# A two-layer hybrid encoder trunk: the output projection's second weight sum moved to VectorE, two stored gates fetched earlier, and three attention steps moved

## The chip, the cores and the metric

The kernel runs on one core of one Trainium2 chip. The metric is the device time of one launch in microseconds: the median of three runs. Beside it stands one execution under the hardware profiler, from which all rows of the profile come. A core has five engines, each of which works through its own list of instructions in order: TensorE (PE, with its weight loads as PEld), VectorE (DVE), ScalarE (ACT), GpSimd (POOL) and SyncE (SP), which here only issues DMAs. The engines wait for one another through semaphores. The lists are made ahead of time by a scheduler, from the order in which the code names the operations.

## The reference

The input is x with 512 rows of 1024 numbers. Two layers are applied. Each has a mixer with three branches and one output projection, and then a gated feed-forward block. Cut to what matters here:

```python
h = x @ w_in[l]                                  # 1024 -> all q, k, v and gates
o_a = retention(...)                             # branch 0: chunkwise retention
o_b = chunk_attention(...)                       # branch 1: softmax over a band of chunks, 8 heads of 64
o_c = diff_attention(...)                        # branch 2: softmax 1 - lam * softmax 2, 4 heads
g = sigmoid(gates + b_merge[l])                  # 3 x 1024 gates for each row
merged = g[0] * (o_a @ w_branch_a[l]) + g[1] * (o_b @ w_branch_b[l]) + g[2] * (o_c @ w_branch_c[l])
mix = merged @ w_out[l]
x = layer_norm(alpha * x + mix)
u_gate, u_up = split(x @ w_ffn_in[l])
x = layer_norm(alpha * x + (silu(u_gate) * u_up) @ w_ffn_out[l])
```

All of it is float32.

## The kernel before

**Products.** Each float32 operand is a pair hi and lo of the type float32r, and a product is three matmuls (`mm3`, L122 to L124: hi by hi, lo by hi, hi by lo). Making the pair is work for two engines: ScalarE casts the high half, VectorE subtracts it from the source for the low half (activations: L106/L108 and L112/L114; weights: L154/L155 and L271/L272). A block of weights passes through a staging tile `st` (four buffers) into `wh` and `wl` (three buffers each): blocks are fetched three ahead of use (`AHEAD`), and a block's cast can begin when the block three before it has been used up. A block is 24 matmuls of 512 columns for a unit of the output projection, and 24 or 48 for the others.

**Units.** The mixer is a list of units, `(u_gate(1, 0), [...], [...])` and so on. A unit loads one block of weights, computes two tiles, and calls `between()` after each; each call runs the next group of steps in the unit's lists. Steps named s_ are the small work of the branches. `u_dqk(h)` projects the queries and keys of one head pair of the differential branch, q first, then one group, then k, then the rest of the groups. `u_gate(br, i)` and `u_branch(br, i)` compute two tiles each of gates and branch outputs.

**The branches' steps.** `s_c1(h)` makes the scores of head h of the chunked attention in four PSUM banks (psc, L422/L423), adds a bias table and takes the maximum on VectorE (L437), exponentiates on ScalarE (L439), and normalises on VectorE (L910, L914). `s_c2(h)` transposes the result on TensorE (ptr, L452, ten transposes) and splits it into a pair (cP). `s_c3(h)` multiplies by v (pco, L939), and ScalarE and VectorE read the bank (cos L941, cot L942). `s_d0` to `s_d4` do the same for the differential branch: `s_d0(h, 1)` ends with the difference of the two softmaxes (L979 to L985, dE), `s_d2(h)` transposes dE, `s_d3(h)` multiplies by v, `s_d4(h)` turns the result. The eight PSUM banks rotate: a new tile waits until the tile that held its bank has been read.

**The gates.** A gate tile is th. Those of branch 0 and the pair (2, 0) are computed long before use (`EARLY`), stored to DRAM, and fetched again. In `u_branch` each tile's fetch (L1081) is issued by SP in the unit that uses it, and VectorE then computes (th + 1) * pt (L1083) and adds it to the branch sum (L1087). Sums of four tiles and quarter sums of them (s12, s43, m1, m2: `s_mleft` L294/L295, `s_mright` L304/L305) become the pairs for the output projection.

**The output projection** is done with seven products of quarter matrices instead of eight, called m1, m2, y, v, x, g, h in the order of use. Their weights are sums of quarters of w_out, each quarter 1 MB. Class `Chain` makes the sums along one staging tile `a`: m1 takes the first quarter, and then an accumulate DMA, issued by POOL (`more`, L178), adds the second quarter in place; y takes that sum, a second accumulate adds the fourth quarter; x takes it, a third accumulate adds the third quarter; h takes that. v and m2 load the fourth and third quarters as they are, and g's sum is made apart (`ahead_c`). The accumulate can start only when both ScalarE and VectorE have read `a` for the block before. The residual rows z (8 loads from x, L459) are updated from each product (L1141, L1143); the statistics for the norm follow (L478, L495, L497).

**SP's queue** takes the loads in the order in which the units are written, with weight loads three blocks ahead of use. A load whose staging buffer is not yet free holds up all that is queued behind it.

Of the kernel before, what the change touches and what calls it, by code (L numbers as in the profile page):

```python
# [56 lines left out]
def trunk(ctx, tc, x_in, xT_in, w_in, ret_norm_g, da_norm_g, lq1, lk1, lq2, lk2, w_a, w_b, w_c, b_merge, w_out,  # L57
# [133 lines left out]
    class Chain(Halves):  # L191
# [21 lines left out]
        def v(self):  # L213
            return self.block(self.load(1, 1))

        def h(self):
            return self.block(self.__dict__.pop("a"))

    class Close(Halves):

# [395 lines left out]
    def layer(l):  # L616
# [282 lines left out]
        def s_c1(h):  # L899
            def fn():  # L900
                if h == 0:
                    bias_table(0)
                if h + 1 < CA_HEADS:
                    bias_table(h + 1)
                tb = ctb.pop(h)
                nc.vector.memset(tb[0:64, 0:64], -NEG)
                E = [g(name="cE") for _ in range(3)]
                sums = softmax_num(cqk[h // 2], h % 2, tb, E)
                r = small.tile([P, NT], F32, tag="rec", name="rec")
                nc.vector.reciprocal(r, sums)  # L910
                for nt in range(NT):
                    pk, c = PACK[NT - 1 - nt]
                    e = E[pk][:, c:c + P * (nt + 1)]
                    nc.vector.tensor_scalar_mul(e, e, r[:, nt:nt + 1])  # L914
                cE[h] = E
            return fn

        def s_c2(h):
            def fn():
                cP[h] = triangle("cP")  # L920
                transpose_triangle(cE.pop(h), cP[h])
            return fn

        def s_c3(h):
            def fn():
                p, j = divmod(h, 2)
                if j == 0:
                    ob[p] = g(name="cot")
                o_ = ob[p]
                pT = cP.pop(h)  # L930
                ps = bank("pco")
                for mt in range(NT):
                    b, o = PACK[mt]
                    w = S - P * mt
                    vt, c = v_of(cv, mt, h, 64)
                    hi = (ps[:, P * mt:], vt[:, c:c + P], pT[b].hi[:, o:o + w])
                    lo = (ps[:64, P * mt:], vt[:, c:c + 64], pT[b].lo[:, o:o + w])
                    for x in ((hi, lo) if mt == 0 else (lo, hi)):
                        nc.tensor.matmul(*x, start=mt == 0 and x is hi, stop=mt == NT - 1 and x is hi)  # L939
                t = g(name="cos")  # L940
                nc.scalar.copy(t[:64], ps[64:128])  # L941
                nc.vector.tensor_add(o_[64 * j:64 * j + 64], ps[:64], t[:64])  # L942
                if j:
                    ob[p] = Pair("ob")
                    split(ob[p], o_)
            return fn
# [5 lines left out]
        def u_dqk(h):  # L952
            def fn(wt):
                if "cd" not in tabs:
                    tabs["cd"], tabs["sd"], tabs["mask"] = g(name="cosd"), g(name="sind"), g(name="mask")
                    nc.sync.dma_start(tabs["cd"], rope_da[0])
                    nc.sync.dma_start(tabs["sd"], rope_da[1])
                    nc.vector.memset(tabs["mask"], 0.0)
                    nc.vector.memset(tabs["mask"][0:64, 0:64], -NEG)
                dqk[h] = QK()  # L960
                dqk[h].set_q(rotary(proj_T(xT, wt, 0), tabs["cd"], tabs["sd"], 32), -DA_DH ** -0.5)
                between()
                dqk[h].set_k(rotary(proj_T(xT, wt, P), tabs["cd"], tabs["sd"], 32))
            return [([wcols(DQ + P * h, P), wcols(DK + P * h, P)], KT)], fn
# [99 lines left out]
        def u_gate(br, i):  # L1064
# [3 lines left out]
                    between()  # L1068
            return [(cols_of(W, GATE + D * br, br, i), KT)], fn

        def u_branch(br, i):
            w = (w_a, w_b, w_c)[br][l]
            nk = w.shape[0] // P

            def fn(wt):
                act = (oa, ob, oc)[br]
                for j, d in enumerate(tiles(br, i)):
                    t = th.pop((br, d))
                    if (br, i) in EARLY:
                        away, t = t, g(name="th")  # L1080
                        nc.sync.dma_start(t, away)  # L1081
                    ps = proj_T(act, wt, P * j, nk=nk)
                    nc.vector.scalar_tensor_tensor(t, t, 1.0, ps, op0=ALU.add, op1=ALU.mult)  # L1083
                    if br == 0:
                        acc[d] = t
                    else:
                        nc.vector.tensor_add(acc[d], acc[d], t)  # L1087
                    if br == 2 and j == 0:
                        q = mq[d] = Quarters()
                        pr = HalfPair("m1")  # L1090
                        split(pr, acc[d][:, q.A], scale=0.5)
                        q.put("m1", pr, q.A)
                    elif br == 2:
                        pr = Pair("m2")
                        split(pr, acc[d], scale=0.5)
                        mq[d - 4].put("m2", pr, q.A)
                        mq[d - 4].put("h", pr, q.B)
                    between()
            return [(cols_of(w, 0, br, i), nk)], fn
# [53 lines left out]

        def out_items():

            hv = Chain(w_out[l], 0, 4)
            w = {}

            def it(name, i, hf, op, last=False, whole=False):
                def fn(wt):  # L1160
                    on = {"x": "m1", "g": "m1", "h": "m1", "v": "y"}.get(name, name)
                    for j in range(2):
                        t = 2 * i + j
                        w[on, j] = product(mq, name, j, wt, w.pop((on, j), None))
                        plus(x1, t, hf, w[on, j], op, last)
                        if name in ("m2", "v", "h"):
                            w.pop((on, j))
                        if whole:
                            x1["n"].normalise(t)
                        between()  # L1170
                return [getattr(hv, name)], fn

            add, sub = ALU.add, ALU.subtract
            return {"c": hv.ahead_c, "m1": it("m1", 0, 0, add), "m2": it("m2", 0, 0, add, True), "y": it("y", 1, 1, add),
                    "x": it("x", 0, 1, sub, True, True), "v": it("v", 0, 1, add), "g": it("g", 1, 1, sub, True),
                    "h": it("h", 1, 0, add, True, True)}
# [25 lines left out]
        for (specs, fn), *groups in start + [  # L1202
            (w["x"], [p["a"]]), (u_gate(0, 3),), (w["g"],), (w["h"], [p["c"]]),
            (p["m1"], [s_dh(0)]), (p["y"], [], [s_r1(0)]), (p["v"], [s_dh(1)]), (p["m2"], [], [s_r1(1)]),
            (p["x"], [q["a"]]), (u_rqk(rq, RQ, 1),), (p["g"], [q["c"]]), (p["h"],),
            (q["m1"], [], [s_r2(0)]), (q["y"], [s_r2(1)]), (u_rqk(rk, RK, 1), [], [s_r3(0)]),
            (q["v"], [s_dh(2)], [s_r3(1)]), (q["m2"], [], [s_r1(2)]), (q["x"], [s_dh(3)]), (u_cqk(0), [], [s_r1(3)]), (q["g"],), (q["h"],),
            (u_gate(2, 0), [s_r2(2)], [s_r2(3), s_r3(2)]), (u_cqk(1), [s_r3(3)] + c(0)[0], c(0)[1]),
            (u_branch(0, 0), c(1)[0] + [v_back(cv)], c(1)[1]), (u_branch(0, 1), *c(2)), (u_cqk(2), *c(3)),
            (u_branch(0, 2), *c(4)), (u_cqk(3), *c(5)), (u_branch(0, 3), *c(6)),   # L1210
            (u_dqk(0), [s_c3(5), s_c2(6), s_c1(7)]), (u_gate(1, 0), [s_c3(6)], [s_c2(7)]),
            (u_dqk(1), [v_back(dv), s_c3(7)] + d(0)[1]), (u_branch(1, 0), *d(1)),
            (u_gate(1, 1), [], d(2)[0] + d(2)[1]), (u_branch(1, 1), *d(3)), (u_dqk(2),),
            (u_gate(1, 2), *d(4)), (u_branch(1, 2), *d(5)), (u_dqk(3),),
            (u_gate(1, 3), *d(6)), (u_branch(1, 3), *d(7)), (u_gate(2, 1), [s_d4(2)], [s_d2(3)]),
            (u_gate(2, 2), [s_d3(3)], [rows_in, s_d4(3)]),
            (u_branch(2, 0), [], [s_mleft(0)]), (u_branch(2, 1), [], [s_mleft(1)]), (u_gate(2, 3), [s_mright(0)], [s_mright(1)]),
            (u_branch(2, 2), [o["c"]]), (u_branch(2, 3), [], [s_mleft(2), s_mleft(3)]),
            (o["m1"], [s_mright(2)]), (o["m2"], [s_mright(3)]), (o["y"],), (o["v"],), (o["x"], [norm_rows]),
            (o["g"], [], [s_turned(0)]), (o["h"],),  # L1220
        ]:
            item(specs, fn, *groups)
# [237 lines left out]
```

## Time and profile before

| | |
|---|---|
| median of 3 runs | 1918.4 us (1915.35 to 1918.87) |
| the profiled execution, its own time | 1918.99 us |
| its span, first to last instruction | 1917.2 us |
| mean granted TensorE clock | 0.990 |
| DVE busy | 1390.2 us, 73% |
| mean weight cast (L271) and low half (L272) of a 1 MB block | 1911 and 2290 ns |

A row of a timeline gives the start in us, the duration in us, the engine, the line of the kernel, the operation, the tiles (out<-in), their shapes and a count; in brackets stands how long the engine had been idle before it, and what it had waited for. A row of the waits gives the engine and what waited, the releaser, then the sum in us, the number of waits and the longest. A row of the windows gives the window, its length, and busy time with the number of instructions for PE, PEld, DVE, ACT and POOL, then the granted clock, the DMA share and GB/s. Times named for the first layer have their twin some 952 us later in the second (the wait for m, for one, is 6.6 us in one and 6.7 in the other).

### The profile page before, as it was taken

The numbers are of one execution on the slowest core, as the hardware profiler recorded it, in microseconds if no ns is written. First come the engines' busy times: TensorE is split into PE (matmuls) and PEld (weight loads), VectorE is DVE, ScalarE is ACT, GpSimd is POOL, SyncE is SP. The second block draws the span as 40 slices with busy tenths as digits, with TensorE's granted clock in tenths as the row PEclk, the third lists the DMA queues.
The fourth block names the chain that finished last, engine by engine and source line by source line (L and its number), as shares of the span: only waits on it lengthen the run. The fifth ranks groups of instructions, "written<-read, shape, count | busy, mean of one in ns | idle before, by whom it ended". The sixth has DMA issues, their size and how long they took to land. (4 is left out here: it accounts for less than half of the span.)

```text
span 1917.2 us, 23308 instructions
## 1 busy us (share of the span) xinstructions
PE 1868.9 (97%) x8754; PEld 1553.1 (81%) x8754; DVE 1390.2 (73%) x2117; ACT 989.9 (52%) x1593; POOL 136.5 (7%) x153
## 2 busy tenths in 40 slices
PE   9999999999988999999999999999999899999998
PEld 7788888788877888888878888887888678888886
DVE  6777756667568776888686867566675687768886
ACT  5545554666534544654264555455665345455541
POOL 2000000000001000010020000000000011000100
PEclk9999999999999999999999999999999899999999
DMA  9584453232357676797386745522323576777871
GB/s 291 170 269 132 121 171 115 67 121 77 102 151 176 155 196 181 183 227 203 129 231 202 230 110 151 178 83 83 110 66 116 142 189 158 195 178 208 209 197 45
DMA packets 235937, 302.89 MB, mean 158 GB/s; under 512 B 8756, under 2 KB 127632, under 8 KB 235824
## 3 DMA queue, kind: packets, MB, share of 16 engines
q1 hardware_dynamic: 205488, 242.25, 38.4%
q0 software_dynamic: 30336, 59.15, 18.0%
q8 instruction: 69, 1.13, 0.2%
q14 instruction: 44, 0.36, 0.1%
HBM read 279.29 MB, written 22.07 MB: 157 GB/s over the span
## 5 line engine op out<-in xcount | busy, mean ns | idle before, releaser
L272 DVE TENSOR_TENSOR wl<-st,wh 128x2048 fp32r<-128x2048 f32 x140 | 320.3, 2290 | 121.4 <-ACT wh L271 120.8
L122 PE MATMUL pt<-xTh,wh 128*128 128x512 f32 x960 | 378.7, 395 | 9.4 <-DVE cot L942 7.4
L271 ACT CAST wh<-st 128x2048 fp32r<-128x2048 f32 x140 | 267.0, 1911 | 226.5 <-PE pf L124 109.5
L124 PE MATMUL pt<-xTh,wl 128*128 128x512 f32 x960 | 375.1, 391 | 0.0
L123 PE MATMUL pt<-xTl,wh 128*128 128x512 f32 x960 | 374.9, 391 | 0.0
L155 DVE TENSOR_TENSOR wl<-st,wh 128x1024 fp32r<-128x1024 f32 (+1 forms) x188 | 200.5, 1084 | 68.1 <-ACT wh L154 47.5
L154 ACT CAST wh<-st 128x1024 fp32r<-128x1024 f32 (+1 forms) x188 | 172.1, 941 | 115.3 <-issue 42.1
L122 PEld LDWEIGHTS pt<-xTh,wh 128*128 128x128 f32 x960 | 180.9, 189 | 47.2 <-DVE cot L942 7.7
L124 PEld LDWEIGHTS pt<-xTh,wl 128*128 128x128 f32 x960 | 180.9, 188 | 38.4
L123 PEld LDWEIGHTS pt<-xTl,wh 128*128 128x128 f32 x960 | 181.2, 189 | 36.6 <-DVE xTl L112 0.2
L122 PE MATMUL pf<-wh,xTh 128*128 128x512 f32 x336 | 132.6, 395 | 1.5 <-ACT rph L106 0.8
L123 PE MATMUL pf<-wl,xTh 128*128 128x512 f32 x336 | 131.3, 391 | 0.6 <-DVE wl L272 0.6
L124 PE MATMUL pf<-wh,xTl 128*128 128x512 f32 x336 | 130.3, 390 | 0.0
L123 PE MATMUL pf<-wl,s12h 128*128 128x512 f32 x256 | 100.0, 391 | 3.7 <-DVE wl L272 3.7
L122 PE MATMUL pf<-wh,s43h 128*128 128x512 f32 x256 | 100.0, 391 | 2.1 <-DVE rs L497 2.1
L122 PE MATMUL pf<-wh,s12h 128*128 128x512 f32 x256 | 100.3, 394 | 1.7 <-ACT s12h L108 1.7
L124 PE MATMUL pf<-wh,s12l 128*128 128x512 f32 x256 | 99.7, 390 | 0.0
L124 PE MATMUL pf<-wh,s43l 128*128 128x512 f32 x256 | 99.7, 389 | 0.0
L123 PE MATMUL pf<-wl,s43h 128*128 128x512 f32 x256 | 99.6, 389 | 0.0
L746 ACT COPY tc<-pf 128x512 f32<-128x512 f32 x84 | 48.5, 589 | 81.1 <-PE pf L124 76.3
L122 PEld LDWEIGHTS pf<-wh,xTh 128*128 128x128 f32 x336 | 63.1, 188 | 17.5 <-ACT rph L106 1.6
L123 PEld LDWEIGHTS pf<-wl,xTh 128*128 128x128 f32 x336 | 63.1, 188 | 13.5 <-DVE wl L272 1.3
(327 smaller groups left out, 3683.4 us busy)
## 6 DMA issues: line engine op xcount, KB each, us to landing
st<-in_w_in SPq DMA_DIRECT2D x53, 1024.0 KB, 6.2
st<-in_w_ffn_in SPq DMA_DIRECT2D x38, 1024.0 KB, 5.9
st<-in_w_in SPq DMA_DIRECT2D x48, 512.0 KB, 4.9
st<-in_w_ffn_in POOLq DMA_DIRECT2D x20, 1024.0 KB, 10.0
st<-in_w_ffn_out SPq DMA_DIRECT2D x20, 1024.0 KB, 7.4
st<-in_w_ffn_out POOLq DMA_DIRECT2D x16, 1024.0 KB, 9.1
st<-in_w_in POOLq DMA_DIRECT2D x12, 1024.0 KB, 10.9
st<-in_w_ffn_in SPq DMA_DIRECT2D x24, 512.0 KB, 5.6
```

Of the source, the lines that this page charges most:

```text
L122: nc.tensor.matmul(ps, lh, rh, start=start, stop=False, skip_group_check=onto)
L123: nc.tensor.matmul(ps, lh, rl, start=False, stop=False, skip_group_check=onto)
L124: nc.tensor.matmul(ps, ll, rh, start=False, stop=stop, skip_group_check=onto)
L154: return [nc.scalar.copy(self.hi[:, a:b], self.st[:, a:b]), nc.vector.tensor_sub(self.lo[:, a:b], self.st[:, a:b], f(self.hi[:, a:b]))]
L155: nc.vector.tensor_sub(self.lo[:, a:b], self.st[:, a:b], f(self.hi[:, a:b]))]
L271: nc.scalar.copy(self.hi, st)
L272: nc.vector.tensor_sub(self.lo, st, f(self.hi))
L746: nc.scalar.copy(t[to, j], ps)
```

## The change

Three edits, each of which acts once in each layer.

1. The output projection uses `Mixed` in place of `Chain`. y's block no longer starts an accumulate DMA. v's block (the fourth quarter, loaded anyway) is cast for v as before, and VectorE then adds it to `a` (a new `tensor_add` of 128x2048 elements). x takes `a` and starts the accumulate of the third quarter, as before. The sums are the same.
2. The gates of (2, 0) are fetched by a new step `gates_in(2, 0)` in the first group of `u_gate(2, 1)`, two blocks earlier than in `u_branch(2, 0)`; `u_branch` keeps its fetch for branch 0 only.
3. `s_c1(7)` moves from between u_dqk(0)'s q and k to behind k. `s_d2(0)` moves from the end of `u_gate(1, 1)` to the middle of `u_branch(1, 1)`, and `s_d3(0)` from the middle of `u_branch(1, 1)` to the middle of `u_dqk(2)`.

```diff
+    class Mixed(Chain):
+        def v(self):
+            self.d = self.load(1, 1)
+            b = self.block(self.d)
+            nc.vector.tensor_add(self.a, self.a, self.__dict__.pop("d"))
+            return b
+
+        def x(self):
+            return self.take(1, 0)
+
+        def y(self):
+            return self.block(self.a)
...
+        def gates_in(br, i):
+            def fn():
+                for d in tiles(br, i):
+                    t = g(name="th")
+                    nc.sync.dma_start(t, th[br, d])
+                    th[br, d] = t
+            return fn
...
-                    if (br, i) in EARLY:
+                    if br == 0:
                         away, t = t, g(name="th")
                         nc.sync.dma_start(t, away)
...
-            hv = Chain(w_out[l], 0, 4)
+            hv = Mixed(w_out[l], 0, 4)
...
-            (u_dqk(0), [s_c3(5), s_c2(6), s_c1(7)]), (u_gate(1, 0), [s_c3(6)], [s_c2(7)]),
+            (u_dqk(0), [s_c3(5), s_c2(6)], [s_c1(7)]), (u_gate(1, 0), [s_c3(6)], [s_c2(7)]),
...
-            (u_gate(1, 1), [], d(2)[0] + d(2)[1]), (u_branch(1, 1), *d(3)), (u_dqk(2),),
+            (u_gate(1, 1), [], d(2)[1]), (u_branch(1, 1), [s_d2(0)], d(3)[1]), (u_dqk(2), [s_d3(0)]),
...
-            (u_gate(1, 3), *d(6)), (u_branch(1, 3), *d(7)), (u_gate(2, 1), [s_d4(2)], [s_d2(3)]),
+            (u_gate(1, 3), *d(6)), (u_branch(1, 3), *d(7)), (u_gate(2, 1), [gates_in(2, 0), s_d4(2)], [s_d2(3)]),
```

The lists of the engines move as follows. A row gives its number, the line, the operation, the tiles and the shape; the changed kernel's lines stand 16 to 24 lower in the file, so that its L453 is L437 of before, its L405 to L407 are L389 to L391, its L288 is L272. All pieces are of the first layer.

First, the attention steps. VectorE at the last chunked scores, before (cot and obl are the result of s_c3(5), cPl and cP the transposed tiles of s_c2(6), cE the softmax of s_c1(7)):

```order
361 L942 TENSOR_TENSOR cot<-pco,cos 64x512
362 L112 TENSOR_TENSOR obl<-cot,obh 128x512
363 L112 TENSOR_TENSOR cPl<-ptr,cPh 128x512 x2
364 L112 TENSOR_TENSOR cP<-ptr,cP 128x256
365 L437 ISA cE,mx<-psc,tb 128x512
366 L437 ISA mx 128x1
367 L437 ISA cE,mx<-psc,tb 128x384
368 L437 ISA mx 128x1
```
And in the change (rot, sw and kl belong to the rotation and split of u_dqk(0)'s k, wl to the next block's weights):

```order
363 L112 TENSOR_TENSOR cPl<-ptr,cPh 128x512 x2
364 L155 TENSOR_TENSOR wl<-st,wh 128x512
365 L112 TENSOR_TENSOR cP<-ptr,cP 128x256
366 L405 TENSOR_TENSOR rot<-pt,cosd 128x512
367 L406 TENSOR_TENSOR sw<-sw,sind 128x512
368 L155 TENSOR_TENSOR wl<-st,wh 128x512
369 L407 TENSOR_TENSOR rot<-rot,sw 128x512
370 L112 TENSOR_TENSOR kl<-rot,ks 64x512
371 L453 ISA cE,mx<-psc,tb 128x512
372 L453 ISA mx 128x1
```
The first cE stood right behind the transposed tiles; now the rotation and split of k stand between them. TensorE at the differential branch's transposes, before:

```order
1857 L124 MATMUL pt<-xTh,wl 128x512
1858 L452 MATMUL ptr<-ident,dE 128x128 x6
1859 L422 MATMUL psc<-ks,qs 128x512
1860 L423 MATMUL psc<-kl,qs 128x512
1861 L452 MATMUL ptr<-ident,dE 128x128 x4
1862 L422 MATMUL psc<-ks,qs 128x384
```
And in the change, from the last score matmul of s_d0(1, 0) to the transposes:

```order
1874 L124 MATMUL pt<-obh,wl 128x512
1875 L122 MATMUL pt<-obh,wh 128x512
1876 L123 MATMUL pt<-obl,wh 128x512
1877 L124 MATMUL pt<-obh,wl 128x512
1878 L468 MATMUL ptr<-ident,dE 128x128 x10
1879 L122 MATMUL pt<-obh,wh 128x512
```
The ten transposes were the first thing behind the gate unit's last matmul and were mixed with the next scores; now the scores and the twelve matmuls of the first branch tile stand ahead of them.

Second, SP's queue, from the last load ahead of the output projection's, before (st<-in_w_out are the quarters of m1, g, m2 and v in this order, th the two stored gates):

```order
120 L174 DMA st<-in_w_out 128x4x512
121 L459 DMA z<-in_x 128x512 x8
122 L1081 DMA th<-th_2_0_2087 128x512
123 L174 DMA st<-in_w_out 128x4x512 x2
124 L1081 DMA th<-th_2_4_2164 128x512
125 L174 DMA st<-in_w_out 128x4x512
```
And in the change:

```order
120 L1091 DMA th<-th_2_0_2087 128x512
121 L1091 DMA th<-th_2_4_2164 128x512
122 L174 DMA st<-in_w_out 128x4x512
123 L475 DMA z<-in_x 128x512 x8
124 L174 DMA st<-in_w_out 128x4x512 x3
```
The two gates stood behind one and behind three loads of w_out; now both stand ahead of all of them and of z.

Third, VectorE in the output projection, from v's low half to x's, before:

```order
611 L272 TENSOR_TENSOR wl<-st,wh 128x2048
612 L114 SCALAR_TENSOR_TENSOR s12l<-sa,s12h 128x512
613 L294 TENSOR_TENSOR sa<-th 128x256
614 L1143 TENSOR_TENSOR z<-z,pf 128x512
615 L295 TENSOR_TENSOR sa<-sa,th 128x256
616 L478 BN_STATS bn<-z 128x6
617 L1143 TENSOR_TENSOR z<-z,pf 128x512
618 L114 SCALAR_TENSOR_TENSOR s12l<-sa,s12h 128x512
619 L304 TENSOR_TENSOR sb<-th,sa 128x256
620 L305 TENSOR_TENSOR sb<-th 128x256
621 L478 BN_STATS bn<-z 128x6
622 L272 TENSOR_TENSOR wl<-st,wh 128x2048
```
And in the change:

```order
609 L288 TENSOR_TENSOR wl<-st,wh 128x2048
610 L114 SCALAR_TENSOR_TENSOR s12l<-sa,s12h 128x512
611 L310 TENSOR_TENSOR sa<-th 128x256
612 L226 TENSOR_TENSOR st<-st 128x2048
613 L311 TENSOR_TENSOR sa<-sa,th 128x256
614 L1167 TENSOR_TENSOR z<-z,pf 128x512 x2
615 L494 BN_STATS bn<-z 128x6 x2
616 L114 SCALAR_TENSOR_TENSOR s12l<-sa,s12h 128x512
617 L320 TENSOR_TENSOR sb<-th,sa 128x256
618 L321 TENSOR_TENSOR sb<-th 128x256
619 L288 TENSOR_TENSOR wl<-st,wh 128x2048
```
The sum into `a` (L226) stands between two subtractions of the quarter sums, ahead of z's updates and of x's low half. POOL's list loses the second of its three accumulates into `a`.

## The prediction

> **What bounds the kernel now.** I read the page's first lines, then the waits of TensorE, then the clock by windows, and last the timelines at each long wait.
>
> ```profile
> span 1917.2 us, 23308 instructions
> PE 1868.9 (97%) x8754; PEld 1553.1 (81%) x8754; DVE 1390.2 (73%) x2117; ACT 989.9 (52%) x1593; POOL 136.5 (7%) x153
> ...
> PE pf L122 <- ACT m L108: 13.4, 2, 6.7
> PE pt L122 <- DVE cot L942: 7.4, 2, 3.7
> PE pf L123 <- DVE wl L272: 4.3, 3, 1.9
> PE ptr L452 <- DVE dE L985: 2.8, 2, 1.4
> ...
> PE pf L122 <- ACT s12h L108: 1.7, 2, 0.9
> ```
>
> TensorE is busy 97% of the span, so time can only be won where it waits or where its clock is low. The waits come in pairs, one per layer: the second number is the count, the third the longest. Four places carry them: 6.6 us at the output projection's m1, 3.7 us after the last chunked scores, 1.4 us at the differential branch's transposes, and 0.9 + 1.9 us at the output projection's x. All four lie where the change cuts.
>
> A wait costs more than itself, as the windows show (PE busy is the second column, the granted clock the one before the DMA share):
>
> ```profile
> 369.90:373.30 3.40, 3.40 (x9) 2.66 (x10) 2.90 (x7) 1.84 (x5) 0.00 (x0) 0.50 0.00 0
> 421.08:424.49 3.41, 1.87 (x10) 0.95 (x9) 2.64 (x9) 3.13 (x7) 0.00 (x0) 1.00 0.20 64
> 424.50:427.90 3.40, 3.40 (x14) 3.15 (x13) 3.10 (x5) 1.35 (x3) 0.00 (x0) 0.50 0.00 0
> 565.40:572.00 6.60, 0.00 (x0) 0.00 (x0) 4.49 (x7) 2.88 (x4) 0.00 (x0) 0.69 1.00 241
> 572.10:578.00 5.90, 5.90 (x14) 4.64 (x15) 5.90 (x9) 1.43 (x3) 0.70 (x1) 0.50 0.07 26
> 605.39:608.81 3.42, 2.17 (x10) 1.49 (x9) 3.42 (x5) 0.79 (x1) 1.30 (x1) 1.00 0.18 49
> ```
>
> After the waits of 3.7 and 1.4 us the clock is 0.50 for 3.4 us, and after the 6.6 us wait still for 5.9 us of work. Half a clock loses half of that time: 1.7, 1.7 and 2.9 us. A stretch of 3.4 us with 1.87 us of work was followed by the low clock; one with 2.17 us was not (nor the pair of waits at x). So my estimate is that more than about 1.4 us of idleness within one such stretch costs a further 1.7 us.
>
> **Place 1, the last chunked scores (s_c1(7)) moved behind u_dqk(0)'s k.**
>
> ```profile
> 363.52 1.28 PE L452 MATMUL ptr<-ident,cE 128*128 128x128 f32 x10
> ...
> 365.79 0.27 PE L423 MATMUL psc<-kl,qs 128*128 128x128 f32 x1
> 369.77 0.72 PE L122 MATMUL pt<-xTh,wh 128*128 128x512 f32 x1 [3.70 <-DVE cot L942]
> ...
> 369.03 0.68 DVE L942 TENSOR_TENSOR cot<-pco,cos 64x512 f32<-64x512 f32 x1
> ...
> 371.01 1.29 DVE L112 TENSOR_TENSOR cPl<-ptr,cPh 128x512 fp32r<-128x512 f32 x2
> ...
> 372.55 0.68 DVE L437 CUSTOM_DVE_ANT_0 cE<-psc,tb 128x512 f32<-128x512 f32 x1
> ...
> 375.81 1.28 DVE L914 TENSOR_SCALAR cE<-cE,rec 128x128 f32<-128x128 f32 x4
> ...
> 389.13 1.25 PE L452 MATMUL ptr<-ident,cE 128*128 128x128 f32 x10
> ```
>
> The ten transposes are issued by about 364.6, the scores take four PSUM banks until 366.06, and then k's 24 matmuls find no bank until VectorE has read pco at 369.03 (it waits there behind a rotation). With the scores behind them, k's matmuls start at 364.6 in a bank that is free. By the nearest block, 24 matmuls in 5.45 us (24 x 0.227, the step of rows at full clock such as 551.86 and 552.08 below), they end near 370.0, and the scores then find pco's bank read at 369.7. The 3.70 us and its 1.7 us of low clock go. Two things are late next. The gate's first bank is a transposed tile that cPl reads until 371.7 (half of the row of 1.29), against a TensorE ready at 371.35: 0.4 us. And in VectorE's new list the k rotation and one kl stand ahead of the first cE: ScalarE's copies and the rotation end near 377, the chain from the first cE (372.55) to the end of the last (377.09) is 4.5 us, and the moved kl and ACT cast add some 3, so the transposes can start at 384.4 to 385.0 against a ready TensorE at 384.1: 0.6 us. Gain 3.7 + 1.7 - 0.4 - 0.6 = 4.4 us; bounds 0 (the chain is 4 us longer than I count) and 5.4.
>
> **Place 2, s_d2(0) and s_d3(0) half a unit later.**
>
> ```profile
> 421.78 0.18 DVE L979 RECIPROCAL rec<-sums 128x4 f32<-128x4 f32 x1 [1.49 <-ACT dE L439]
> ...
> 422.46 1.94 DVE L985 SCALAR_TENSOR_TENSOR dE<-dE,rec 128x128 f32<-128x128 f32 x4
> ...
> 422.87 1.47 PE L452 MATMUL ptr<-ident,dE 128*128 128x128 f32 x6 [1.38 <-DVE dE L985]
> ```
>
> The transposes come at 421.49 and the exponentials are normalised from 422.46 to 424.40. In the new order eight score matmuls (some 1.3 us, as from 364.6 to 366.06) and twelve branch matmuls (2.7 us) stand ahead, so they come near 425.3 and find dE done or 0.2 us away. Gone are the 1.38, the 1.7 of low clock, and some 0.6 of the drip through (six transposes in 1.47 us here, ten in 1.28 at place 1): 3.5 us; bounds 1.4 (the low clock returns) and 3.9. s_d3(0), moved with it, only uses the transposes 24 matmuls later.
>
> **Place 3, the wait for m1.**
>
> ```profile
> 541.77 1.13 SPq L1081 DMA_DIRECT2D th<-th  x1
> ...
> 551.72 0.69 DVE L1083 SCALAR_TENSOR_TENSOR th<-th,pt 128x512 f32<-128x512 f32 x1 [5.90 <-DMA th<-th]
> ...
> 558.64 2.29 DVE L272 TENSOR_TENSOR wl<-st,wh 128x2048 fp32r<-128x2048 f32 x1 [0.20 <-ACT wh L271]
> ...
> 561.24 1.28 POOL L178 DMA_DIRECT2D st<-in_w_out  x1 [20.46 <-DVE wl L272]
> ...
> 569.75 1.90 ACT L271 CAST wh<-st 128x2048 fp32r<-128x2048 f32 x1 [3.20 <-DMA st<-in_w_out]
> 571.55 0.41 ACT L108 ACTIVATE m<-th 128x256 fp32r<-128x256 f32 x1
> ...
> 572.02 0.80 PE L122 MATMUL pf<-wh,m 128*128 128x512 f32 x1 [6.62 <-ACT m L108]
> ...
> 551.86 0.39 PE L124 MATMUL pt<-xTh,wl 128*128 128x512 f32 x1
> 552.08 0.39 PE L122 MATMUL pt<-och,wh 128*128 128x512 f32 x1
> ```
>
> Read backwards: TensorE needs m, which stands behind y's cast on ScalarE; the cast needs the accumulate DMA of 561.24; that needs m1's wl, which stands on VectorE behind 5.90 us of idleness for the second stored gate. Its fetch was issued at 541.77, behind w_out loads that wait for staging buffers. Two blocks earlier it lands long before. Then m1's cast is bound by its weight buffer, free when the gate block's last matmul ends at 552.15: cast 1.90 to 554.05, wl 2.29 to 556.4, POOL 0.35 later, the DMA 8.5 (561.24 to 569.75) to 565.25, y's cast to 567.1, m to 567.5. TensorE's wait starts at 565.39: 2.1 us instead of 6.6, and with four chances in five more than 1.4 of it in one stretch, so 1.3 of low clock instead of 2.9. Gain 4.5 + 1.6 = 6.1; bounds 0 and 9.5.
>
> The Trainium skill, "DMA: Bandwidth & Descriptors", Anatomy of one DMA — SWDGE (gpsimd) path, fits 2.0 us plus bytes/436e3, an estimate of 4.4 us for this megabyte; by it the wait for m would vanish and the sum be near 1886. The 8.5 us between the two rows above speak against it.
>
> **Place 4, x's sum by VectorE.**
>
> ```profile
> 578.37 1.91 ACT L271 CAST wh<-st 128x2048 fp32r<-128x2048 f32 x1 [3.15 <-PE pf L124]
> ...
> 586.03 1.91 ACT L271 CAST wh<-st 128x2048 fp32r<-128x2048 f32 x1 [5.21 <-DMA st<-in_w_out]
> ...
> 590.37 2.27 DVE L272 TENSOR_TENSOR wl<-st,wh 128x2048 fp32r<-128x2048 f32 x1
> ...
> 588.51 0.50 PE L122 MATMUL pf<-wh,s12h 128*128 128x512 f32 x1 [0.93 <-ACT s12h L108]
> 592.70 0.50 PE L123 MATMUL pf<-wl,s12h 128*128 128x512 f32 x1 [1.85 <-DVE wl L272]
> ...
> L233 DVE TENSOR_TENSOR st<-st x12: 2283/2292/2293, 61.9 to 1740.5; 128x2048 f32<-128x2048 f32 x12
> ```
>
> x's cast waits 5.21 us for the second accumulate, and TensorE stands 0.93 + 1.85 us. That DMA goes; an add of 2.29 us (the kernel's own sums elsewhere) takes its place. With m1 done at 570.4 (567.5 plus twelve matmuls, 2.8): v's cast to 572.4, its wl to 575.0, the add to 578.2, x's cast to 580.2, then s12h, s12l, sb twice, and x's wl 582.15 to 584.45. TensorE reaches x's weights at 579.9 and waits 0.25 and then 2.3 us: 2.55 for 2.78. Queued behind the add on VectorE are z's sums and the splits of s12 and s43, about 0.5 later than now. The 2.3 us lie together, where 1.85 fell over two stretches, so the low clock is likely: 1.4. So this place loses 0.5 + 1.4 - 0.2 = 1.7 us against a later m1; bounds +2.8 and -4.
>
> **Sum**: 4.4 + 3.5 + 6.1 - 1.7 = 12.3 per layer, and 0.7 back, since what of m1's low clock falls after m1's end only delays TensorE's arrival at x, where it waits anyway: 13.0. Two layers: 26. The profiled run's own time is 1918.99 us, 0.6 above the median of 1918.4; 1919 - 26 = **1893 us**.
>
> **The rivals.**
>
> A, the clock holds (0.19): waits near 2 us do not lower it. Then 2 x (1.3 + 1.4) more is won: about 1888; 1884 if the accumulate also lands 2 us sooner. Against it stands the stretch with 1.87 us of work, for it only the one with 2.17. The Trainium skill, "TensorE: Matmul & The Clock Gate", Part 1, states this rule: the clock falls after an idle window of about 3.4 us; this trace lowered it after a wait of 1.38 us.
>
> B, the out projection gives nothing (0.10): the cast of m1, or x's chain through three engines, takes up what the earlier gate wins. Places 1 and 2 remain: 1919 - 2 x 7.9 = 1903. For it: y's cast still stands ahead of m, and the x chain has no slack.
>
> C, the wait of place 1 goes to the transposes (0.10): VectorE's chain comes 4 us later than I count. 1919 - 2 x (3.5 + 4.4) = 1903.
>
> D, slower (0.06): the gate fetches now stand ahead of w_out's first load and z in SP's queue; if their slots come free late, VectorE waits for them at the same instruction as now and m1's load behind them is late too. Each microsecond past 541.77 is one more at m1; with 7.9 won at places 1 and 2 it decides from an issue at 549.7. At 552.15, with the weight buffer, it is 10.4 - 7.9 = 2.5 per layer: 1924. Against it: the loads that take such slots now went out together:
>
> ```profile
> 518.89 4.88 SPq L459 DMA_DIRECT2D z<-in_x  x8
> ```
>
> E (0.03): new small waits eat all, within 0.2% of 1919, which is what a measurement of this kernel can tell from no change.
>
> **How the numbers follow.** The forecast has 0.52. Faster is forecast, A, B and C: 0.91; same 0.03; slower 0.06. The range runs from A with a quicker transfer, places 1 and 2 nearer their upper ends, 1882, to past B and C, 1905.
>
> **What would show it.** In the changed profile: no wait on cot and a first k matmul right behind the ten transposes; under 1 us at c2(7); none over 0.3 us at dE; VectorE's wait for th gone, TensorE's wait for m near 2 us, x's wait on wl near 2.3 us, each followed by 3.4 us at 0.50 or not, which decides A. A wait for m still above 5 us, or a DMA wait at x's cast, would make the forecast wrong.

## The result and the profile after

| | median us | lowest to highest | runs |
|---|---|---|---|
| before | 1917.11 | 1915.35 to 1918.87 | 4 |
| after | 1886.88 | 1885.41 to 1890.11 | 4 |

The ratio is 0.9845 (95% interval 0.9827 to 0.9862): 30.2 us faster, where 26 was forecast. The median of 1886.88 stands 6.1 us under the forecast of 1893 and nearer to rival A's 1888: 4.2 us because the change gave more, and 1.9 because the kernel before took 1917.11 and not 1919. The profiled execution of the changed kernel took 1890.11 us, 28.9 less than that of before; the ledger below is made against these 28.9.

The head of the page, and TensorE's waits (what it waited for, then us in total, times, longest):

```profile
span 1888.3 us, 23317 instructions
PE 1860.3 (99%) x8754; PEld 1547.7 (82%) x8754; DVE 1392.3 (74%) x2119; ACT 989.1 (52%) x1593; POOL 133.7 (7%) x151
```

```profile
PE pf L123 <- DVE wl L288: 5.8, 3, 2.0
PE pf L122 <- ACT m L108: 3.7, 2, 2.0
PE pf L122 <- DVE z L1167: 2.3, 1, 2.3
```

The waits for cot (7.4 us) and for dE (2.8) have left the list. The wait for m fell from 13.4 to 3.7 us. x still waits for its low half, wl (twice 2.0 of the 5.8 us), but no more for s12h. VectorE does two instructions more, and GpSimd's transfers two fewer: the sum is where the diff put it.

TensorE's timeline at places 1 and 2 (start, duration, line, tiles, and in brackets the idle time before and who ended it):

```profile
363.66 1.28 PE L468 MATMUL ptr<-ident,cE 128*128 128x128 f32 x10
364.69 0.48 PE L122 MATMUL pt<-xTh,wh 128*128 128x512 f32 x1
...
371.90 0.50 PE L122 MATMUL pt<-xTh,wh 128*128 128x512 f32 x1 [0.28 <-DVE cPl L112]
...
384.20 1.26 PE L468 MATMUL ptr<-ident,cE 128*128 128x128 f32 x10
...
420.42 1.25 PE L468 MATMUL ptr<-ident,dE 128*128 128x128 f32 x10
```

k's first matmul stands directly behind the ten transposes; the wait that is late next is the 0.28 us for cPl. The transposes of c2(7) and of dE have no bracket: nothing is waited for there, and the ten of dE go through in one piece.

The chain of place 3, then of place 4, from the timelines of VectorE, GpSimd, ScalarE and TensorE:

```profile
545.48 2.29 DVE L288 TENSOR_TENSOR wl<-st,wh 128x2048 fp32r<-128x2048 f32 x1 [0.44 <-ACT wh L287]
548.07 1.28 POOL L178 DMA_DIRECT2D st<-in_w_out  x1 [16.03 <-DVE wl L288]
556.83 1.90 ACT L287 CAST wh<-st 128x2048 fp32r<-128x2048 f32 x1 [5.25 <-DMA st<-in_w_out]
558.63 0.41 ACT L108 ACTIVATE m<-th 128x256 fp32r<-128x256 f32 x1
559.10 0.50 PE L122 MATMUL pf<-wh,m 128*128 128x512 f32 x1 [1.97 <-ACT m L108]
...
567.30 2.28 DVE L226 TENSOR_TENSOR st<-st 128x2048 f32<-128x2048 f32 x1
569.69 1.91 ACT L287 CAST wh<-st 128x2048 fp32r<-128x2048 f32 x1 [5.05 <-DVE st L226]
573.49 2.28 DVE L288 TENSOR_TENSOR wl<-st,wh 128x2048 fp32r<-128x2048 f32 x1
575.82 0.50 PE L123 MATMUL pf<-wl,s12h 128*128 128x512 f32 x1 [1.97 <-DVE wl L288]
```

VectorE's idle time for th ahead of m1's wl has gone; the block starts 8.7 us earlier than before (554.25 against 562.96), and with 8.7 taken off, the forecast's times are 548.1 for GpSimd's accumulate, 556.5 for y's cast and 575.75 for the end of x's wl. The rows say 548.07, 556.83 and 573.49 + 2.28 = 575.77.

Ledger of TensorE from start to start of the same matmuls, in us:

| stretch | before, layer 1 | after, layer 1 | won, layer 1 | won, layer 2 | forecast |
|---|---|---|---|---|---|
| transposes of c2(6) to those of c2(7): place 1 | 25.61 | 20.54 | 5.1 | 4.8 | 4.4 |
| to m1's first matmul: place 2 | 173.83 | 170.05 | 3.8 | 3.8 | 3.5 |
| m1 to m2: place 3 | 15.17 | 7.71 | 7.5 | 7.6 | 6.1 |
| m2 to h: place 4 | 34.38 | 34.97 | -0.6 | 0.0 | -1.0 |

The four places win 15.7 + 16.2 = 32.0 us. The feed-forward part gives 3 back in this execution (a wait of 1.83 us for wl in layer 1 behind an accumulate of 10.3 us, with a low clock after it, less 0.95 won in layer 2); the same kernel run again below does not show that wait. Nor does it show the 2.3 us for z at g (L1167, layer 1 alone): it has two such waits of at most 1.0 instead.

What the waits do to the clock, by windows (the second number is the stretch's length, the third TensorE's busy time, the one before the DMA share the granted clock):

```profile
554.98:558.39 3.41, 2.15 (x10) 1.45 (x8) 1.73 (x3) 1.56 (x1) 0.00 (x0) 1.00 1.06 341
558.39:561.80 3.41, 2.71 (x12) 2.17 (x13) 2.73 (x3) 1.18 (x3) 0.00 (x0) 1.00 0.07 26
...
572.05:575.46 3.41, 1.80 (x8) 1.05 (x6) 3.41 (x5) 1.61 (x2) 0.00 (x0) 1.00 0.96 292
575.46:578.87 3.41, 3.05 (x13) 2.52 (x14) 3.38 (x7) 1.54 (x3) 1.28 (x1) 1.00 0.77 245
...
592.53:595.94 3.41, 3.41 (x10) 2.63 (x9) 2.95 (x3) 0.00 (x0) 3.41 (x2) 0.50 0.92 253
...
1497.06:1500.47 3.41, 1.64 (x8) 0.98 (x7) 1.25 (x3) 2.74 (x3) 0.00 (x0) 1.00 0.74 286
1500.47:1503.88 3.41, 3.41 (x17) 2.80 (x17) 3.41 (x4) 0.94 (x1) 0.00 (x0) 1.00 0.02 5
1514.13:1517.54 3.41, 1.44 (x6) 0.87 (x6) 3.38 (x4) 2.43 (x2) 0.51 (x1) 1.00 0.75 281
1517.54:1520.95 3.41, 3.41 (x9) 2.64 (x9) 3.41 (x5) 0.63 (x1) 0.78 (x1) 0.50 0.78 163
```

x waits 1.97 us for wl in both layers. In layer 1 the wait lies across the border at 575.46, 1.61 + 0.36, and the clock stays at 1.00; in layer 2 all of it falls into one stretch, which is left with 1.44 us of work, and the next runs at 0.50. The waits for m leave 2.15 and 1.64 us of work in their stretches, and the stretches behind them run at 1.00: they cost no clock. The stretch from 592.53 follows the wait of 2.34 us for z at g in layer 1 and runs at 0.50.

### The profile page after: what moved, and what is told of

It is laid out like the page before. It is cut to its first block, busy times and chain, and to the rows that moved or that the text cites. A ratio compares the mean times of both kernels' runs of the same rounds, so it can differ in the third digit from the quotient of the medians.

```text
span 1888.3 us, 23317 instructions
## 1 busy us (share of the span) xinstructions
PE 1860.3 (99%) x8754; PEld 1547.7 (82%) x8754; DVE 1392.3 (74%) x2119; ACT 989.1 (52%) x1593; POOL 133.7 (7%) x151
## 5 line engine op out<-in xcount | busy, mean ns | idle before, releaser
L288 DVE TENSOR_TENSOR wl<-st,wh 128x2048 fp32r<-128x2048 f32 x140 | 320.1, 2289 | 124.2 <-ACT wh L287 123.6
```

The lines of the kernel that those rows point to most:

```text
L288: nc.vector.tensor_sub(self.lo, st, f(self.hi))
```

## Experiments: each part alone

Four of these runs take the kernel before and make one edit of the change alone, and a fifth makes two; each was timed beside the kernel before on its own chip.

**Only the last chunked scores moved.**

```diff
-            (u_dqk(0), [s_c3(5), s_c2(6), s_c1(7)]), (u_gate(1, 0), [s_c3(6)], [s_c2(7)]),
+            (u_dqk(0), [s_c3(5), s_c2(6)], [s_c1(7)]), (u_gate(1, 0), [s_c3(6)], [s_c2(7)]),
```

> Only the last chunked scores move (s_c1(7) behind k); all else is as before. Theory (the gains of the places add up, each where it is): TensorE's 3.7 us wait on cot and the 3.4 us at half clock behind it are gone, the transposes of s_c2(7) come 5 us sooner without a wait of their own, in both layers: 10 us less, about 1907. Rival (the gain of a place is given back at the next wait, since the out projection's chain hangs on DMAs): under 4 us less, and the wait for m grows from 6.6 to over 9 us.

Measured 1906.57 against 1916.31, ratio 0.9949 (0.9932 to 0.9966): 9.7 us. The wait for cot is gone and the wait for m is still 6.4 us, so place 1 is worth what its ledger says (5.1 + 4.8) and doesn't lean on the others.

**Only s_d2(0) and s_d3(0) moved.**

```diff
-            (u_gate(1, 1), [], d(2)[0] + d(2)[1]), (u_branch(1, 1), *d(3)), (u_dqk(2),),
+            (u_gate(1, 1), [], d(2)[1]), (u_branch(1, 1), [s_d2(0)], d(3)[1]), (u_dqk(2), [s_d3(0)]),
```

> Only s_d2(0) and s_d3(0) move. Theory: the 1.4 us wait on dE and its half clock go, 3.8 us a layer, 7.6 in all, about 1909.5; the wait for m stays 6.6. Rival: given back at m, under 3 us less.

Measured 1911.40, 0.9976 (0.9966 to 0.9985): 4.9 us instead of 7.6, with an interval from 2.9 to 6.5. The two profiled executions differ by 7.2 us, and its own place wins 3.8 us per layer in them. From m2 to h, which the edit doesn't touch, it loses 1.0 and 0.7 us, and the windows at x show how:

```profile
587.43:590.84 3.41, 1.55 (x7) 1.00 (x6) 3.41 (x4) 2.35 (x2) 0.25 (x1) 1.00 0.34 132
590.84:594.25 3.41, 3.41 (x10) 2.63 (x9) 3.41 (x6) 0.63 (x1) 1.03 (x1) 0.50 0.49 68
```

The wait of 1.86 us for x's wl, which in the kernel before fell over two stretches and cost no clock, now falls into one, and the next runs at half the clock. What an edit upstream wins can so be less or more than its own wait by 1.7 us, by where it pushes a later wait. But this doesn't explain the 2.7 us that are missing, since the same execution wins 1.2 and 1.0 us from m1 to m2, where the clock is low for 6.8 us per layer and not for 10.2.

What does bear on it is that the 3.8 us hold the 1.7 of the low clock, and the kernel before doesn't always have it. In the runs below that leave this place alone, and in the run above, the wait for dE is again 1.4 us in both layers, but a stretch at 0.50 follows in two of six. With only the sum moved it follows in neither, and in layer 1 the wait, from 422.54 to 423.93, falls over two stretches:

```profile
419.71:423.12 3.41, 2.84 (x13) 2.02 (x11) 1.85 (x9) 3.36 (x11) 0.00 (x0) 1.00 0.86 290
423.12:426.53 3.41, 2.44 (x15) 1.88 (x16) 3.38 (x8) 2.67 (x5) 0.00 (x0) 1.00 0.00 0
```

From c2(7) to m1 such a layer takes 172.2 us and not the 173.8 of the profile of before, so that the move is worth 2.2 us there and not 3.8: between 4.4 and 7.6 us in all. How often the low clock comes in the executions without a profile isn't known.

**Both moves together**, to see if the loss is a fixed one:

> Only the moved steps, scores and differential branch together. Theory (gains of places 1 and 2 add, 5.0 and 3.8 a layer by the changed kernel's trace): 17.6 us less than before, about 1899. The two moves alone gave 9.7 and 4.9, 14.6 together, which would be 1902: if it is that, 1.5 us a layer are given back at the waits for m and x, where the low clock falls otherwise.

Measured 1900.45, 0.9921 (0.9906 to 0.9936): 15.4 us, 2.2 short of the sum of the places, 0.8 over the sum of the two alone. The interval, 12.3 to 18.0 us, holds both, so this run doesn't settle whether the gains add up in full. The remaining waits lie at m (13.3 us) and at x, as before.

**Only the gates fetched early** (the sums stay with the accumulating transfers):

```diff
+        def gates_in(br, i):
...
-                    if (br, i) in EARLY:
+                    if br == 0:
...
-            (u_gate(1, 3), *d(6)), (u_branch(1, 3), *d(7)), (u_gate(2, 1), [s_d4(2)], [s_d2(3)]),
+            (u_gate(1, 3), *d(6)), (u_branch(1, 3), *d(7)), (u_gate(2, 1), [gates_in(2, 0), s_d4(2)], [s_d2(3)]),
```

> Only the two stored gates are fetched earlier; the out projection still makes its second sum by the accumulate DMA. Theory: the fetch alone ends VectorE's idleness, and the wait for m falls from 6.6 to about 2 us. x's weights: y's low half ends 4.9 us after y's cast begins, the accumulate lands 9 us later, so x's cast begins about 14 us after y's, while in the changed kernel it began 12.9 us after y's cast and then waited for s12 on VectorE; the low half of x comes within 1 us of the changed kernel's. So 7 us less a layer, about 1903. Rival (VectorE's sum is what frees x): the wait for m falls, but x's wait grows by 4 us or more, so under 8 us less in all, above 1909.

Measured 1900.83, 0.9923 (0.9908 to 0.9938): 15.5 us. Its waits:

```profile
PE pf L122 <- ACT s12h L108: 5.7, 2, 2.9
PE pf L122 <- ACT m L108: 3.2, 2, 1.6
```

The wait for m falls from 13.4 us to what it is in the whole change, with no help from the sum. x's weights, which stand behind the second accumulate, are waited for as long as before: 5.7 us, against 1.7 + 4.3 (of whose three waits one lies elsewhere).

**Only the sum on VectorE.**

```diff
-            hv = Chain(w_out[l], 0, 4)
+            hv = Mixed(w_out[l], 0, 4)
```

> Only x's sum is made by VectorE; the gates are still fetched late. Theory: m still waits 6.6 us for y's accumulate; v's low half, a split, the add and x's cast follow v's cast, and x's cast begins near 586.0, where the accumulate landed before: within 2 us of 1917. Rival (the second accumulate is what TensorE pays for): x's waits of 0.9 and 1.9 us go and 5 us or more are won, about 1911.

Measured 1916.66, 1.0003 (0.9993 to 1.0012): nothing. Its waits:

```profile
PE pf L122 <- ACT m L108: 12.5, 2, 6.4
...
PE pf L123 <- DVE wl L288: 4.0, 2, 2.0
PE pf L122 <- DVE z L1159: 3.1, 2, 2.3
```

No transfer stands ahead of x's cast any more, and the same few microseconds are waited for x's wl and for z, behind the add. The four alone sum to 9.7 + 4.9 + 15.5 - 0.4 = 29.7 us; the change as a whole gave 30.2.

## Experiments: what the sum is worth beside the rest

**The change without the sum, and the change again**, on the same chip:

```diff
-            hv = Mixed(w_out[l], 0, 4)
+            hv = Chain(w_out[l], 0, 4)
```

> The change without the sum on VectorE: early gates and moved steps, but x's sum by the accumulate DMA again. Theory (the early gates win the out projection's time, the sum on VectorE next to nothing): x's weights wait for a transfer of about 8.8 us instead of an add, which here end within 1 us of one another; x's wait near 2.9 us for 2.0, so 0 to 2 us above the changed kernel in all, 1887 to 1889. Rival (the two edits need each other): x's wait takes back what m gained, 6 us or more above the changed kernel, over 1893.

> The changed kernel itself, for comparison on the same chip: 1886 to 1888. The wait of 1.83 us in the feed-forward block and the 2.3 us one at g were of transfers that happened to be long: theory, they are not there again in the same size; rival, they belong to the change and come again.

Measured 1885.84 (0.9840, 0.9826 to 0.9853) without it, 1885.56 (0.9840, 0.9827 to 0.9854) with it. The waits of the output projection without the sum:

```profile
PE pf L122 <- ACT s12h L108: 5.7, 2, 3.0
PE pf L122 <- ACT m L108: 3.1, 2, 1.5
...
PE pf L122 <- DVE z L1151: 1.1, 2, 0.6
PE px L518 <- DVE z L500: 1.1, 2, 0.5
```

And with it:

```profile
PE pf L123 <- DVE wl L288: 4.0, 2, 2.0
PE pf L122 <- ACT m L108: 3.3, 2, 1.8
PE px L534 <- DVE z L516: 1.9, 2, 1.0
PE pf L122 <- DVE z L1167: 1.6, 2, 1.0
```

5.7 + 3.1 + 1.1 + 1.1 = 11.0 against 4.0 + 3.3 + 1.9 + 1.6 = 10.8 us, and with the sum another 0.6 for rs, the norm's statistics. The sum shortens the wait at x by 1.7 and lengthens those for z, which stand behind it on VectorE, by 1.3. With the clock counted in, the stretches from m2's first matmul to h's last take 81.5 us in both layers together without the sum and 82.5 with it. With the gates early or late, the first edit of the change moves waits and wins nothing.

**What the add itself costs: left out, done twice, done by GpSimd.**

```diff
-            nc.vector.tensor_add(self.a, self.a, self.__dict__.pop("d"))
+            self.__dict__.pop("d")
```

> The changed kernel with the new add on VectorE left out and no transfer in its place, so x's and h's weights lack the fourth quarter: what x's sum costs at all. Theory (in this stretch VectorE's list is full, so the add costs its own 2.3 us at x less what the later waits take back): x's wait of 2.0 us shrinks to under 1, 1 to 2 us a layer less, 1882 to 1884. Rival (the add lies in VectorE's idle time and costs nothing): 1885 to 1886.5.

```diff
+            nc.vector.tensor_add(self.a, self.a, self.d)
             nc.vector.tensor_add(self.a, self.a, self.__dict__.pop("d"))
```

> The changed kernel with the add made twice (x's and h's weights then have the fourth quarter twice). Theory: the second add lies wholly on x's chain, x waits 4.3 us for 2.0 and the low clock comes each time: 2.3 to 4 us a layer more, 1890 to 1893.5. Rival (hidden): under 1 us more, 1885 to 1887.

Left out: 1876.90, 0.9798 (0.9784 to 0.9813). Twice: 1893.75, 0.9884 (0.9867 to 0.9900). These ran on another chip, so the ratios are compared: beside the change's 0.9840, one add less is 0.0042 of 1916 = 8.0 us, and one more 0.0044 = 8.4: about 4 us per layer for an instruction of 2.29. Left out, it gave more than expected; twice, it came out just above the upper end of what was expected. Left out, the rows at x are:

```profile
566.90 1.92 ACT L287 CAST wh<-st 128x2048 fp32r<-128x2048 f32 x1 [3.00 <-PE pf L124]
568.85 2.29 DVE L288 TENSOR_TENSOR wl<-st,wh 128x2048 fp32r<-128x2048 f32 x1
```

x's cast now waits for TensorE to free its weight buffer, not for VectorE, and wl follows at once; no wait for x is left. With two adds the wait at x is

```profile
PE pf L123 <- DVE wl L289: 9.2, 2, 4.6
```

4.6 us per layer and a low clock behind it. An add more thus costs its 2.29 in the wait, and the clock that the longer wait loses; an add less takes the whole wait of 2.0 away, 1.0 of the 3.5 us of later waits for z, and what clock the wait cost. That the add lies on the path that bounds this stretch is so shown from both sides. It lies there in two ways: x's cast waits for its result (5.05 us, the row at 569.69 above), and VectorE works without a gap from 559.1 to 581.2, so that x's wl starts 1.9 us after that cast has ended. The two runs move both at once and don't show what each is worth.

```diff
-            nc.vector.tensor_add(self.a, self.a, self.__dict__.pop("d"))
+            nc.gpsimd.tensor_add(self.a, self.a, self.__dict__.pop("d"))
```

> The changed kernel with the same add made by GpSimd instead of VectorE; the results are the reference's. GpSimd is idle from 548 to 576 us there; no run shows how long it takes for such an add (its 64x512 memset takes 0.52 us). Theory (only VectorE's queue makes the sum dear): `a` is free for the sum when y's low half is done, near 561, and x's cast cannot begin before m2's weight buffer is free, near 567. So an add of up to 5.7 us is hidden, and the time is that with the sum left out, 1877 to 1879; at 8 us it is 2 us a layer more, 1881 to 1883. Rival (VectorE is slowed while GpSimd works beside it, or the add takes over 10 us): 1885 or more.

Measured 1886.83, 0.9845 (0.9831 to 0.9858): nothing won, and the rival came true. GpSimd's row, then VectorE's at the same time:

```profile
563.46 4.94 POOL L226 TENSOR_TENSOR st<-st 128x2048 f32<-128x2048 f32 x1 [12.10 <-DVE wl L288]
```

```profile
563.84 4.84 DVE L310 TENSOR_TENSOR sa<-th 128x256 f32<-128x256 f32 x1
...
572.94 0.41 DVE L310 TENSOR_TENSOR sa<-th 128x256 f32<-128x256 f32 x1
```

The difference of two gates, 0.41 us elsewhere, takes 4.84 us and ends with GpSimd's add. VectorE is held for longer than its own add would have taken, and TensorE's wait turns into one for s12l, twice 2.0 us.

## Experiments: the wait that is left at m

m stands behind y's cast on ScalarE. Here an order between the two is added (the last m ahead of the cast), once with the sum and once with the accumulating transfer in its place (the lines that keep hold of the cast and of the last m are left out here):

```diff
         def y(self):
-            return self.block(self.a)
+            b = self.block(self.a)
+            tc.add_manual_dep(b.cast.ins, self.last_m.ins.name, ...
```

> The changed kernel, with y's cast put behind the last m on ScalarE. Theory: the 2 us that TensorE still waits for m are only m's place behind a cast that waits for a DMA; with m ahead the wait is gone (under 0.3 us), y's weights come in time, and x's wait of 2 us stays, as its chain starts from m1's end: 3.5 to 4 us less than the changed kernel, about 1883. Rival: y's low half is then late and the wait goes on to y or x, 0 to 1 us less.

> The kernel with m first, but x's sum by the accumulate DMA. Theory: once m1 no longer waits, TensorE reaches x 2 us sooner while the accumulate still hangs on y's low half, so x and the s12 behind its cast wait 4 to 6 us instead of 2; here VectorE's sum is worth 4 to 8 us in all, 1887 to 1891. Rival: the sum is worth nothing here either, 1883 to 1885.

With the sum 1884.25 (0.9832, 0.9819 to 0.9846), 1.3 us under the change, whose interval overlaps; without it 1883.48 (0.9827, 0.9814 to 0.9841), 2.1 under it, and every one of its four runs (1881.49 to 1883.73) below every one of the change's (1884.42 to 1886.59). The waits with the sum:

```profile
PE pf L123 <- DVE wl L291: 4.0, 2, 2.0
PE pf L122 <- DVE z L1171: 2.8, 2, 1.6
PE px L537 <- DVE z L519: 1.9, 2, 1.0
PE pf L122 <- ACT wh L290: 1.6, 2, 0.9
```

And without it:

```profile
PE pf L122 <- ACT s12h L108: 7.4, 2, 4.0
PE pf L122 <- DVE mv L505: 1.7, 2, 0.8
```

The wait for m is gone in both, and 10.3 and 9.1 us of waits remain where there were 10.8 and 11.0 (the 0.6 for rs stays with the sum). y's cast now comes after the last m, and TensorE waits for the cast's wh instead, for z longer, or, without the sum, for s12h 0.9 us longer per layer. My expectation of 3.5 to 4 us took a wait at the head of a chain for its length. That the kernel without the sum would be the slower of the two was wrong as well: by its median it is the fastest version here that computes the whole reference.

## Why the prediction was right, and where its sizes were off

**Place 1** held: no wait on cot, k's matmuls behind the transposes, cPl late next. The 0.4 us for cPl were 0.28, and the 0.6 us counted at c2(7) did not come: VectorE's chain was ready in time. Hence 5.1 and 4.8 instead of 4.4. Rival C, in which that chain comes 4 us late, is refuted by the same row.

**Place 2** held, with 3.8 for 3.5 against this profile of before. But the 1.7 us of low clock in it were counted as certain, and the runs with an unchanged place 2 show them in two layers of six; with and without them the move is worth 4.4 to 7.6 us in all, and alone it gave 4.9.

**Place 3** held in its mechanism, and the run with early gates alone shows that it carries the change: y's accumulate, cast and m came within 0.4 us of the forecast, the wait was 1.97 and 1.77 us instead of 2.1. The term of the sum that was mis-sized is the low clock, 1.3 of a forecast gain of 6.1. The estimate that "more than about 1.4 us of idleness within one such stretch" lowers it came from one row, that of the dE transposes; here 1.77 us did not. This is rival A's mechanism at this place, half of what A needs: in layer 2 the wait at x did lower the clock. So A's case held at m in both layers, and the forecast's own at x in one; the median lies near A's 1888 although A held only in part, and 1.9 us of that are the quicker kernel before. The accumulate took 548.07 to 556.83, 8.8 us (8.5 before); the quicker transfer did not come. The Trainium skill, "DMA: Bandwidth & Descriptors", Anatomy of one DMA — SWDGE (gpsimd) path, makes 4.4 us an estimate for it, and the trace disagrees again.

**Place 4** held: the add replaces the transfer at no gain. x's wait was 1.97 us and not 2.55, its low clock came in layer 2 alone, and the place lost 0.6 and 0.0 instead of 1.0. The 0.6 of layer 1 holds a wait that was not forecast, 2.34 us for z at g with a low clock behind it, which the repeat doesn't show. The forecast gave this edit a small loss; the run of the sum alone (1.0003) and the pair with and without it (1885.56 and 1885.84) make it nothing.

Rival C's sum leaves out the 0.7 us that the forecast gives back; with it C comes to 1902, which changes nothing. Rival B (the output projection gives nothing), D (slower, by late gate fetches) and E (new waits eat all) fell: SP issues the two gates first, and early.

```profile
500.91 0.91 SPq L1091 DMA_DIRECT2D th<-th  x2
509.76 0.38 SPq L174 DMA_DIRECT2D st<-in_w_out  x1
```

The last gate was issued at 541.77 before; both now go by 501.8, and w_out's first load at 509.76, 8.7 us earlier than in the kernel before (518.48). That is just what the two moves won ahead of it, so the gates cost the load behind them nothing. The terms that were too small make 2.7 and 3.2 us per layer; the feed-forward's 3 us in the profiled execution hide half of that, so 26 stood against 28.9.

Open: a sum that is neither on VectorE nor in the accumulating transfer, such as one made ahead in a staging buffer of its own, wasn't tried. Nor was an add on VectorE whose result x doesn't use, which would tell the price of its place on the list from that of its place in x's chain.

## What to carry to other kernels

Price a move by the instruction that the whole chain hangs on: here a fetch that stood behind other loads in one queue held VectorE, and through it a weight load, a cast and TensorE, and moving that fetch gave as much as everything else. An operation that replaces a transfer can give nothing where it lands on an engine whose in-order list is already full, as here, where an add of 2.29 us took the place of a transfer of 8.8; leaving the operation out for one run tells its price (2.29 us of work, 4 us of time). And a wait removed at the head of such a list is won only as far as the next wait in it allows, so sum the waits of the whole stretch before and after.

## What the hardware showed that was not expected

**The clock.** In the traces of these kernels the stretches of 3.41 us run on by themselves: in the changed kernel the low ones at 592.53 and 1517.54 lie 271 times 3.413 us apart. In those that held few or none of the 128-column transposes, where TensorE stood idle for up to 1.77 us in one, the next kept the full clock in over 20 cases, and with 1.83 us or more it got 0.50, save for one stretch that kept it at 1.87, one that lost it at 1.78, and one in the first 10 us of a run that lost it at 1.69. Stretches that held 1.2 us or more of these transposes lost it earlier: seven of them with 1.39 to 1.56 us idle, place 2 of the kernel before among them, while those with up to 1.37 kept it. So two equal waits can cost 0 or 1.7 us, by how they fall over the borders. The Trainium skill, "TensorE: Matmul & The Clock Gate", Part 1: The HAM clock gate, gives a free-running window of 3413 ns and a half rate, and both agree with 3.41 us and 0.50 here; it lets the clock fall after an idle window, where these traces lowered it in windows that were still 46% busy, and with transposes 59%.

**VectorE held by GpSimd.** An operation with two inputs in SBUF on VectorE took 4.84 us instead of 0.41 while GpSimd added for 4.94. The Trainium skill, "SBUF — State Buffer", SBUF: two separate sides, has the two engines share a pair of ports by a lock that is kept for the whole instruction; the two rows agree with it.
